# Cutting the last load of a DMA-bound elementwise kernel in two and holding the first store until the larger piece has landed

## The chip, the cores and the metric

The kernel runs on one core of one Trainium2 chip. The metric is device time in microseconds (us) of one execution, the median over the runs. The profile's span starts at the first DMA issue and is about 1.3 us shorter than the device time.

## The reference

Two float32 arrays of 1024 x 4096 are multiplied, and the tanh form of GELU is applied.

```python
def reference(x, y):
    z = x * y
    return (0.5 * z * (1 + np.tanh(np.sqrt(2 / np.pi) * (z + 0.044715 * z ** 3)))).astype(np.float32)
```

That is 2 x 16.78 MB to read and 16.78 MB to write, with one multiply (VectorE) and one activation (ScalarE) per element.

## The kernel before

Every tensor is seen as 128 partitions x 32768 columns. x stays whole in SBUF (the core's own memory; the arrays lie in HBM, the chip's large memory) and is overwritten by the product and then by the result. y goes through a ring of 16384 columns. All DMAs are issued by the sync engine (SP) on one queue, in this order: first half of x, first half of y, second half of x, third quarter of y, last quarter of y, first half of the result, second half of the result. `_hoist` moves the first two loads to the front of the program.

```python
X_LOADS = [(0, 16384), (16384, 32768)]
Y_LOADS = [(0, 16384, 0), (16384, 24576, 0), (24576, 32768, 8192)]   # from, to, place in the ring
STEP = 4096
STORES = [(0, 16384), (16384, 32768)]
...
    _hoist(nc, [load_x(0).ins, load_y(0).ins])
    load_x(1)
    for i in (1, 2):
        nc.sync.wait_ge(sem_mul, (Y_LOADS[i][1] - Y_LOADS[1][0]) // STEP)
        load_y(i)
    # ... per y load and 4096 columns: tensor_mul, then Gelu activation in place ...
    for i, (a, b) in enumerate(STORES):
        nc.sync.wait_ge(sem_act, b // STEP)
        nc.sync.dma_start(out=out_r[:, a:b], in_=xs[:, a:b]).then_inc(sem_o[i], 16)
```

The first store needs only the fourth activation, so it enters the queue while the second half of the loads is still on its way, right behind the last y load.

## Time and profile before

| | kernel before |
|---|---|
| device time, median of 6 runs (range) | 120.86 us (120.66 to 120.92) |
| span of the profiled execution | 119.3 us |
| DMA queue in use | 98.7% of 16 engines' span |
| VectorE busy, ScalarE busy | 35.0 us, 30.2 us |
| bytes moved, mean rate | 50.33 MB, 422 GB/s |

The page's other lines are shown in the prediction. Two more views of the kernel before are used later. First the DMA issues by tensor (count, KB each, median us from issue to landing):

```profile
ys<-in_y_dram SPq DMA_DIRECT2D x2, 4096.0 KB, 21.0
xs<-in_x_dram SPq DMA_DIRECT2D x2, 40.3
out_dram<-xs SPq DMA_DIRECT2D x2, 31.8
```

Then what the sync engine waited for (total us, times, longest):

```profile
SPq L100 <- ACT xs L94: 33.7, 2, 30.4
SPq L105 <- DMA out_dram<-xs: 6.5, 1, 6.5
```

The stores wait for activations only. These two lines do not say whether a store that leaves early is good or bad; the time at which each transfer lands does. I read two kinds of records under the summary views: the **landing records** (one semaphore increment per DMA engine and transfer; I quote the last of the 16) and the **packet records** (start and length of each packet on a DMA engine). A transfer of 128 partitions is eight packets on each of the 16 engines, one per partition.

### The profile page before, as it was taken

How to read it: one execution, taken by the hardware profiler on the slowest of the kernel's cores; microseconds unless marked ns; L12 is line 12 of the kernel's file. 1: busy time of each engine (PE TensorE's matmuls, PEld its weight loads, DVE VectorE, ACT ScalarE, POOL GpSimd, SP SyncE). 2: the span in 40 equal slices, each digit the busy share in tenths (PEclk: the TensorE clock that was granted, in tenths of full speed). 3: DMA queues.
4: the chain of work that ended last, by engine and by line, in shares of the span. 5: the costliest groups of instructions: out<-in, count | busy, mean ns of one | idle time of the engine just before them, and what ended most of it. 6: DMA issues, size and time to landing. Idle time of an engine off the chain costs nothing.

```text
span 119.3 us, 68 instructions
## 1 busy us (share of the span) xinstructions
DVE 35.0 (29%) x8; ACT 30.2 (25%) x9; POOL 0.2 (0%) x4
## 2 busy tenths in 40 slices
DVE  0000000000000199999600049959990000000000
ACT  3000000000000006797790000977479200000000
POOL 0000000000000000000000000000000000000000
DMA  9899888998899889988898989998889888998894
GB/s 352 352 439 615 352 352 352 659 396 352 352 615 439 352 352 483 571 352 352 385 494 352 505 374 494 385 527 352 352 352 703 352 352 352 637 418 352 352 527 176
DMA packets 1008, 50.33 MB, mean 422 GB/s; under 512 B 112, under 2 KB 112, under 8 KB 112
## 3 DMA queue, kind: packets, MB, share of 16 engines
q1 hardware_dynamic: 1008, 50.33, 98.7%
HBM read 33.55 MB, written 16.78 MB: 422 GB/s over the span
## 4 chain that ended last, share of the span: by engine, by line
DMA 53%; DVE 22%; ACT 3%; SPq 0%; issue 0%; DVEq 0%
DMA ys<-in_y_dram 53%; DVE xs L87 22%; ACT xs L94 3%; SPq L66 0%; DVEq L85 0%
## 5 line engine op out<-in xcount | busy, mean ns | idle before, releaser
L87 DVE TENSOR_TENSOR xs<-xs,ys 128x4096 f32<-128x4096 f32 x8 | 35.0, 4420 | 54.5 <-DMA ys<-in_y_dram 54.5
L94 ACT ACTIVATE xs<-xs 128x4096 f32<-128x4096 f32 x8 | 28.9, 3617 | 61.0 <-DVE xs L87 61.0
L94 ACT ACT_TABLE_LOAD x1 | 1.3, 1283 | 1.9 <-PEq L54 1.9
L121 POOL MEMSET const-uint8-127<- 128x1 uint8 x1 | 0.1, 102 | 0.0
L121 POOL MEMSET const-bfloat16-1.0<- 128x1 bf16 x1 | 0.1, 101 | 0.0
L121 POOL MEMSET const-float32-0.0<- 128x1 f32 x1 | 0.1, 98 | 0.2 <-issue 0.2
L121 POOL MEMSET const-float32-1.0<- 128x1 f32 x1 | 0.1, 98 | 0.0
## 6 DMA issues: line engine op xcount, KB each, us to landing
ys<-in_y_dram SPq DMA_DIRECT2D x2, 4096.0 KB, 21.0
xs<-in_x_dram SPq DMA_DIRECT2D x2, 40.3
out_dram<-xs SPq DMA_DIRECT2D x2, 31.8
ys<-in_y_dram SPq DMA_DIRECT2D x1, 40.8
```

The source lines that it names most:

```text
L87: nc.vector.tensor_mul(out=xs[:, c : c + STEP], in0=xs[:, c : c + STEP], in1=ys[:, r + c - a : r + c - a + STEP],).then_inc(sem_mul, 1)
L94: nc.scalar.activation(out=xs[:, c : c + STEP], in_=xs[:, c : c + STEP], func=GELU).then_inc(sem_act, 1)
L121: nc = _bacc.Bacc("TRN2", target_bir_lowering=False, num_devices=1)
```

## The change

The intent: the store must no longer stand in the queue behind the loads, yet the queue must not run empty. So the last y load becomes 6912 + 1280 columns, and the first store is issued when the 6912 have landed; the 1280 columns keep the engines busy while the store is on its way to them.

```diff
-Y_LOADS = [(0, 16384, 0), (16384, 24576, 0), (24576, 32768, 8192)]
+Y_LOADS = [
+    (0, 16384, 0),
+    (16384, 24576, 0),
+    (24576, 31488, 8192),
+    (31488, 32768, 15104),
+]
...
-    for i in (1, 2):
-        nc.sync.wait_ge(sem_mul, (Y_LOADS[i][1] - Y_LOADS[1][0]) // STEP)
+    for i in range(1, len(Y_LOADS)):
+        nc.sync.wait_ge(sem_mul, -(-(Y_LOADS[i][1] - Y_RING) // STEP))
         load_y(i)
...
         for c in range(a, b, STEP):
+            w = min(STEP, b - c)
             # tensor_mul and activation of w columns instead of STEP
             n += 1
+            done[c + w] = n
...
     for i, (a, b) in enumerate(STORES):
-        nc.sync.wait_ge(sem_act, b // STEP)
+        if i == 0:
+            nc.sync.wait_ge(sem_y[-2], 16)
+        nc.sync.wait_ge(sem_act, done[b])
```

More of the change, by code (lines that the diff above doesn't have):

```diff
@@ L75 @@
     load_x(1)
-    for i in (1, 2):
-        nc.sync.wait_ge(sem_mul, (Y_LOADS[i][1] - Y_LOADS[1][0]) // STEP)
+    for i in range(1, len(Y_LOADS)):
+        nc.sync.wait_ge(sem_mul, -(-(Y_LOADS[i][1] - Y_RING) // STEP))
         load_y(i)
     n = 0
+    done = {}
     for i, (a, b, r) in enumerate(Y_LOADS):
@@ L86 @@
         for c in range(a, b, STEP):
+            w = min(STEP, b - c)
             nc.vector.tensor_mul(
-                out=xs[:, c : c + STEP],
-                in0=xs[:, c : c + STEP],
-                in1=ys[:, r + c - a : r + c - a + STEP],
+                out=xs[:, c : c + w],
+                in0=xs[:, c : c + w],
+                in1=ys[:, r + c - a : r + c - a + w],
             ).then_inc(sem_mul, 1)
             n += 1
+            done[c + w] = n
             nc.scalar.wait_ge(sem_mul, n)
             nc.scalar.activation(
-                out=xs[:, c : c + STEP], in_=xs[:, c : c + STEP], func=GELU
+                out=xs[:, c : c + w], in_=xs[:, c : c + w], func=GELU
             ).then_inc(sem_act, 1)
     for i, (a, b) in enumerate(STORES):
-        nc.sync.wait_ge(sem_act, b // STEP)
+        if i == 0:
+            nc.sync.wait_ge(sem_y[-2], 16)
+        nc.sync.wait_ge(sem_act, done[b])
         nc.sync.dma_start(out=out_r[:, a:b], in_=xs[:, a:b]).then_inc(sem_o[i], 16)
```

## The prediction

> **What bounds the kernel now.** I read the page first (its slices and its DMA part), then the chain of work that ended last, then the DMA landings of each tensor, and last the single packet records of the trace.
>
> ```profile
> span 119.3 us, 68 instructions
> DVE 35.0 (29%) x8; ACT 30.2 (25%) x9; POOL 0.2 (0%) x4
> DMA  9899888998899889988898989998889888998894
> q1 hardware_dynamic: 1008, 50.33, 98.7%
> HBM read 33.55 MB, written 16.78 MB: 422 GB/s over the span
> ...
> L87 DVE TENSOR_TENSOR xs<-xs,ys 128x4096 f32<-128x4096 f32 x8 | 35.0, 4420 | 54.5 <-DMA ys<-in_y_dram 54.5
> L94 ACT ACTIVATE xs<-xs 128x4096 f32<-128x4096 f32 x8 | 28.9, 3617 | 61.0 <-DVE xs L87 61.0
> ```
>
> The reader is to see that the 16 DMA engines are in use for 98.7% of the span, while VectorE and ScalarE work under a third of it. The kernel is one DMA queue that is never empty: 33.55 MB in, then 16.78 MB out. The slices look uneven only because whole packets are booked to a slice.
>
> The chain of waits names loads and multiplies, not the stores, and here it misleads about what is worth shortening:
>
> ```profile
> 58.77 21.87 DMA ys<-in_y_dram
> 80.64 0.03 issue
> 80.67 0.02 DVEq L85
> 80.69 0.04 issue
> 80.73 8.77 DVE xs L87 x2
> 89.50 0.02 issue
> 89.53 3.62 ACT xs L94
> ```
>
> The chain stops where the last activation ends, at 89.53 + 3.62 = 93.15 us. The second store is issued then, but the first store still holds the queue, as the landings by tensor show:
>
> ```profile
> L100 SPq DMA_DIRECT2D out_dram<-xs x2: 344/346/348, 62.4 to 93.2; - x2
> DMA to landing us min/median/max: 26.1/31.8/37.6
> ```
>
> The first store lands at 62.4 + 37.6 = 100.0 us, some 6.9 us after the second was issued, so the compute behind the last y load has 6.9 us of slack, and the second store follows without a hole (93.2 + 26.1 = 119.3 us).
>
> What can still be lost is in the queue itself. From the semaphore records, the last of each transfer's 16 landings is at 21.87 (x, first half), 41.21 (y, first half), 60.55 (x, second half), 70.27 (y, third quarter), 80.64 (y, last quarter), 99.97 (store 1) and 119.26 us (store 2). The differences are 19.34, 19.34, 9.72, 10.37, 19.33 and 19.29 us. A half is 8.39 MB and takes 19.34 us, so a quarter should take 9.67. The last y quarter, the one with a store queued right behind it since 62.4 us, takes 10.37: about 0.7 us too long. The packet records say where: a 32 KB load packet takes 1.213 us everywhere, but on all 16 DMA engines the seventh of the eight packets of that last load takes 1.83 to 2.17 us, starting at 76.6 to 77.1 us. The eighth is nearly normal again, and the store's first packets (2.418 us each, as later ones) follow without a gap. So the switch from loads to stores costs 0.6 to 0.95 us on an engine, and it is paid before the loads have ended. The only other loss is the first packet of the run (3.12 us on average against 2.42).
>
> **What the Trainium skill says.** "DMA: Bandwidth & Descriptors", section "Where 436 GB/s comes from", gives a ceiling of 435 GB/s; the stretch from 21.87 to 60.55 us moves 16.78 MB in 38.68 us, 434 GB/s, which agrees: there is nothing to win in the steady rate. The same page, section "Queues, rings and completion order", says that on each engine descriptors of a ring are consumed in order; the landing times above, in issue order, agree. The same page, "Latency and other measured facts", gives about 600 ns to the first byte of a load issued by the sync engine; here the first x load's issue ends at 0.38 us and its first packet starts at 1.00 us on the earliest engine and 1.48 us on the latest, so 0.62 us and more. I found no page that says what a change of direction in a queue costs.
>
> **The change, part by part.**
> 1. *The last y load is cut in two*, 6912 and 1280 columns. Both wait for the fourth multiply, so both are issued at about 58.8 to 59.2 us, behind a queue that is busy until 70.3. Bytes stay the same. Each load is eight packets per engine (one for each partition), so eight more packets. Two 32 KB packets take 2 x 1.213 = 2.426 us against 2.418 for one of 64 KB: 0.008 us per packet, 0.06 us for eight. No wait is added to the loads.
> 2. *Compute.* DVE work is split 4096, 2816 and 1280 in place of 4096 and 4096, the same columns in one more instruction. The 6912-column piece lands near 78.45 us (below), over 2 us before 80.64, so the last activation ends near 90 to 91 us instead of 93.15. All of it is in slack that the first store makes, and worth nothing.
> 3. *The first store waits for the 6912-column landing* instead of leaving at 62.4 us. This is the part that matters. It removes the stretched packet if that comes from the store standing behind the load: minus 0.7 us (10.37 - 9.67). It adds the risk of an empty queue. Packet time of the 6912 piece: 27/64 x 2.418 = 1.02 us, 8 packets, 8.2 us. The packets of the load before it end between 69.25 and 69.9 us according to the engine, so the piece's end at 77.4 to 78.1, and its last landing some 0.35 us later (as now, 80.30 to 80.64): 78.45. The sync engine passes a met wait in about 0.03 us (62.39 to 62.42 now), so the store is issued at 78.5. Its first packets can start 1.00 to 1.48 us later by the one start from an empty queue that the trace has: 79.5 to 80.0 us. Meanwhile the 1280 columns keep an engine busy for 8 x (5/64 x 2.418 + 0.004) = 1.5 us, to 79.0 to 79.6 us. The gap is then some 0.4 us, an estimate. The first store packet from an idle engine may also be slower than a queued one: the first load's was by 0.7 us, and a store reads from SBUF, so I take 0.15.
> 4. *Sum:* -0.7 + 0.06 + 0.4 + 0.15 = -0.1 us by this working. The odd width 1280 is just the length of the path from landing to first packet, which suggests that it was chosen for covering it; I therefore lean further to the gap being nearly closed and take -0.3 us: 120.87 - 0.3 = about 120.6 us.
>
> **The rivals.**
> A. *The switch itself costs what it costs.* If an engine must let its reads from HBM come home before it reads from SBUF, then 0.7 us of loss stays, moved behind the last load, and hides the late arrival of the store. For it: the start of the run shows a loss of the same size, 0.7 us. Against it: the stretched packet is the seventh, not a gap after the eighth. Result: 120.9 us.
> B. *The store comes too late.* The issue path takes its full 1.5 us, the first packet is 0.5 us slow, and nothing of it is covered: -0.7 + 0.06 + 0.5 + 0.5, up to 121.3 us. For it: 1.48 us on the slowest engine is measured.
> C. *The switch is free when the store comes just as the loads run out*, and the 1280 columns cover the path: the whole 0.7 us is won, 120.2 us. The floor for this queue is 119.3 - 0.7 of span, so nothing faster than about 120.1 us is to be had without touching the beginning.
> D. *The compute becomes the bound* through the extra instruction: it would have to eat 6.9 us of slack, and it gets about 2 us more of it. I give this nothing.
>
> **Range and chances.** A, B and C span 120.2 to 121.3, with most of the weight between A and C. I predict 120.6 us, and 120.1 to 121.1 for 8 in 10; runs of one kernel differ by 0.07 us, so noise adds little. Faster by over 2% means under 118.5 us, below the floor worked out above: 0.01. Slower by over 2% means over 123.3 us, a queue empty for more than 2.4 us: 0.02. The rest, 0.97, is within 2%.
>
> **What would show each step right or wrong.** The first store should be issued at 78.5 us and take some 21 us to land instead of 37.6. The seventh-packet stretch should be gone: the 6912-column piece should land 8.2 us after the y load before it, and no load packet should be over its normal length. Between the last 1280-column packet and the first store packet an engine should stand idle for 0 to 0.5 us; 0.7 us or more there speaks for A or B, and a first store packet well over 2.42 us for a slow start. If the stretch appears in the 6912 piece although no store is queued, then the store was not its cause. The second store must still be issued before the first lands, and land 19.3 us after it. The prediction is wrong in kind if the time is outside 120.1 to 121.1 us: below, if the steady rate of the loads or stores changes; above, if the queue stands empty for more than a microsecond.

## More of the kernel before

The record marks every execution reported here as fast, that is, not slowed, at a granted clock of 1.00. The experiments ran in four groups on four chips (e0 to e3; the widths; e8 to e10; e12). Each group had the kernel before beside it, with medians of 120.86, 120.91, 120.82 and 120.85 us, and the ratios are against these.

## The result

The changed kernel takes **120.13 us** (median of 6 runs, 120.05 to 120.39) against 120.86 us. The ratio is 0.9946, with a 95% interval of 0.9933 to 0.9959. Ratios here are the mean time of one kernel's fast runs over that of the other's fast runs of the same rounds, so they are not quite the ratio of the quoted medians. 0.9946 means 0.65 us saved (0.0054 x 120.86). This is inside the predicted range, but at its lower end.

The page of the changed kernel, to be held against the first fence of the prediction:

```profile
span 118.7 us, 73 instructions
DVE 34.9 (29%) x9; ACT 30.2 (25%) x10; POOL 0.2 (0%) x4
q1 hardware_dynamic: 1152, 50.33, 98.6%
HBM read 33.55 MB, written 16.78 MB: 424 GB/s over the span
```

Bytes and busy times are the same, there are 144 packets more (128 data packets and 16 semaphore writes for one more DMA), and the span is 0.6 us shorter. The share of 98.6% against 98.7% does not show where the time was saved: a packet that is held up counts as busy.

What the sync engine waited for, and the stores' issue and landing times, in the changed kernel:

```profile
SPq L110 <- DMA ys<-in_y_dram: 16.2, 1, 16.2
SPq L110 <- ACT xs L102: 11.7, 1, 11.7
...
L110 SPq DMA_DIRECT2D out_dram<-xs x2: 344/346/347, 78.5 to 90.6; - x2
DMA to landing us min/median/max: 20.9/24.5/28.1
```

The first store now waits 16.2 us for the y piece and leaves at 78.5 instead of 62.4 us. It then needs 20.9 us to land, not 37.6, because only the 1280 columns are in front of it.

The DMA issues of the changed kernel, for the y loads:

```profile
ys<-in_y_dram SPq DMA_DIRECT2D x1, 4096.0 KB, 20.2
ys<-in_y_dram SPq DMA_DIRECT2D x1, 3456.0 KB, 19.9
ys<-in_y_dram SPq DMA_DIRECT2D x1, 640.0 KB, 21.0
```

The landing records tell where the time went. The duration of a transfer is its last landing minus that of the transfer before it in the queue:

| transfer | before, lands at | duration | changed, lands at | duration |
|---|---|---|---|---|
| x, first half | 21.87 | | 21.75 | |
| y, first half | 41.21 | 19.34 | 41.08 | 19.33 |
| x, second half | 60.55 | 19.34 | 60.43 | 19.35 |
| y, third quarter | 70.27 | 9.72 | 70.14 | 9.71 |
| y, last quarter (both pieces) | 80.64 | **10.37** | 80.04 | **9.90** |
| store 1 | 99.97 | 19.33 | 99.39 | 19.35 |
| store 2 | 119.26 | 19.29 | 118.69 | 19.30 |

Of the 0.57 us between these two executions, 0.47 lie in the last quarter of y and 0.12 in the first landing, in which the two kernels do the same; a second profiled execution of the changed kernel (e0) had 22.09 us there. So the real gain lies in one place, where a queue of loads turns into a queue of stores.

### The profile page after: what moved, and what is told of

Its sections match the earlier page's. It is cut to its first block, busy times and chain, and to the rows that moved or that the text cites. A ratio compares the mean times of both kernels' runs of the same rounds, so it can differ in the third digit from the quotient of the medians.

```text
span 118.7 us, 73 instructions
## 1 busy us (share of the span) xinstructions
DVE 34.9 (29%) x9; ACT 30.2 (25%) x10; POOL 0.2 (0%) x4
## 3 DMA queue, kind: packets, MB, share of 16 engines
q1 hardware_dynamic: 1152, 50.33, 98.6%
## 4 chain that ended last, share of the span: by engine, by line
DMA 51%; DVE 18%; ACT 6%; issue 0%; SPq 0%; DVEq 0%
DMA ys<-in_y_dram 51%; DVE xs L94 18%; ACT xs L102 6%; SPq L71 0%; DVEq L91 0%
## 5 line engine op out<-in xcount | busy, mean ns | idle before, releaser
L94 DVE TENSOR_TENSOR xs<-xs,ys 128x4096 f32<-128x4096 f32 (+2 forms) x9 | 34.9, 3946 | 52.8 <-DMA ys<-in_y_dram 52.8
L102 ACT ACTIVATE xs<-xs 128x4096 f32<-128x4096 f32 (+2 forms) x9 | 28.9, 3235 | 58.5 <-DVE xs L94 58.5
```

The costliest lines, as they stand in the source:

```text
L94: nc.vector.tensor_mul(out=xs[:, c : c + w], in0=xs[:, c : c + w], in1=ys[:, r + c - a : r + c - a + w],).then_inc(sem_mul, 1)
L102: nc.scalar.activation(out=xs[:, c : c + w], in_=xs[:, c : c + w], func=GELU).then_inc(sem_act, 1)
```

## The experiments

Theory 1: a store that stands in the queue behind the loads holds their last packets up by 0.7 to 0.8 us, and the late store avoids it. Theory 2: the cut itself helps. Theory 3 (rival A of the prediction): turning from loads to stores costs this anyway. The column "last quarter" is the duration of the last y quarter by landing records, as above; undisturbed it should take 9.67 us, half of a half's 19.34.

| run | time, us | ratio (95%) | last quarter, us |
|---|---|---|---|
| kernel before | 120.86 | | 10.37 |
| e0, change repeated | 120.06 | 0.9935 (0.9923 to 0.9947) | 9.74 |
| e1, cut only | 120.77 | 0.9995 (0.9983 to 1.0007) | 10.36 |
| e2, uncut, store waits for the last y | 121.46 | 1.0052 (1.0040 to 1.0064) | 9.70 |
| e3, uncut, store waits for the third y | 120.87 | 1.0002 (0.9990 to 1.0014) | 10.45 |
| last piece of 768 columns | 120.90 | 1.0003 (0.9984 to 1.0022) | 9.94 |
| last piece of 1536 | 120.03 | 0.9933 (0.9918 to 0.9948) | 9.76 |
| last piece of 2048 | 120.00 | 0.9929 (0.9914 to 0.9945) | 9.82 |
| last piece of 2560 | 120.02 | 0.9928 (0.9911 to 0.9944) | 9.84 |
| e8, one more change of direction | 120.96 | 0.9999 (0.9972 to 1.0026) | 9.45 |
| e9, copy SBUF to SBUF in between | 125.16 | 1.0352 (1.0320 to 1.0385) | 10.72 |
| e10, copy HBM to HBM in between | 125.20 | 1.0356 (1.0324 to 1.0388) | 9.70 |
| e12, small early SBUF copy | 121.08 | 1.0012 (0.9998 to 1.0026) | 10.44 |

All outputs are right.

### e0: the changed kernel again

No edit; it was run beside the three below.

> The changed kernel itself, run on the same chip as the three experiments beside it, so that they have it for comparison. Every theory: 120.1 us, ratio to the kernel before 0.994 to 0.996; no load packet over its normal length before the first store; the loads end 9.9 us after the third y quarter.

It took 120.06 us, and the last quarter 9.74 us. On its engines the pause between the last load packet and the first store packet was 0.32 us on average in the packet records (0.18 in the first profiled execution). The pause is zero on the engine that ends its loads last. No load packet of the last quarter was long here (at most 1.03 us). In the first profiled execution some 27 KB packets took up to 1.18 us instead of 1.02, but at 70 to 75 us, far from the border; the engine that ended last lost 0.23 us there, which accounts for its 9.90 us.

### e1: the cut alone

```diff
     for i, (a, b) in enumerate(STORES):
-        if i == 0:
-            nc.sync.wait_ge(sem_y[-2], 16)
         nc.sync.wait_ge(sem_act, done[b])
```

> The last y load is cut into 6912 and 1280 columns, but the first store leaves at 62.4 us as in the kernel before. Theory 1 (the loss comes from the store standing in the queue behind the last load): the loss is back, 120.8 to 120.95 us, and some load packet near 77 us is 0.6 to 0.9 us too long. Theory 2 (the cut itself helps, by small last packets or earlier compute, and the store's wait does nothing): 120.1 us, no long packet. It also tells where the long packet lies: by count, it is the seventh of the eight 5 KB packets; by time, it is one that begins 1 to 2.4 us before the loads end, thus the last or last but one 27 KB packet.

It took 120.77 us, the time of the kernel before; the interval of the ratio includes 1. The DMA issues of e1 show the early store again, and the last piece half a microsecond slower than in the changed kernel (21.5 against 21.0):

```profile
ys<-in_y_dram SPq DMA_DIRECT2D x1, 640.0 KB, 21.5
xs<-in_x_dram SPq DMA_DIRECT2D x2, 40.4
out_dram<-xs SPq DMA_DIRECT2D x2, 33.1
```

The first 5 KB packets, which take 0.20 us in the changed kernel, take up to 0.65 us here, and some of the last 27 KB packets up to 1.43 instead of 1.02; the final four or so 5 KB packets are normal again. So the stall has a place in time, not in the count of packets. It begins 1.3 to 2.8 us before an engine's loads would have ended; the lengths of the packets do not bound it more closely. Theory 2 is out: the cut by itself wins nothing.

### e2: the wait alone

```diff
     for i, (a, b) in enumerate(STORES):
+        if i == 0:
+            nc.sync.wait_ge(sem_y[-1], 16)
         nc.sync.wait_ge(sem_act, b // STEP)
```

> The loads of the kernel before, uncut, and the first store waits until the last y load has landed. Theory 1: the long packet is gone (last y quarter 9.7 us instead of 10.37), but the queue is empty from landing plus issue: landing 0.35 us after the last packet, issue, and about 0.9 us to the first store packet as in the changed kernel (78.54 issue, 79.4 first packet), so a hole of 1.2 to 1.3 us; 120.86 - 0.7 + 1.25 = 121.4 us. Theory 3 (the change of direction costs 0.7 us anyway, hidden in the changed kernel by nothing): the hole is 1.3 us and the first store packet or the load still shows the 0.7 us, 122.1 us.

121.46 us, as theory 1 had it (121.4). The chain of e2 and its stores' landings:

```profile
58.79 21.21 DMA ys<-in_y_dram
...
L102 SPq DMA_DIRECT2D out_dram<-xs x2: 343/346/348, 80.0 to 92.5; - x2
DMA to landing us min/median/max: 20.8/24.2/27.6
```

The last y load takes 21.21 us from issue to landing, in place of 21.87, so the stall is gone. In exchange the queue is empty: the engines finish their loads at 79.0 to 79.6 us, the landing is complete at 80.00, the store is issued at 80.02, and its first packets start at 80.86 to 81.01. The mean pause of an engine is 1.68 us. This run also gives two sizes cleanly: **0.84 to 0.99 us from issue to first packet**, and 0.4 us from a load's last packet to its landing. A first store packet takes 2.45 us, nearly the usual 2.42.

### e3: a store that is issued later, but still early

```diff
     for i, (a, b) in enumerate(STORES):
+        if i == 0:
+            nc.sync.wait_ge(sem_y[-2], 16)    # loads uncut: the third y quarter
         nc.sync.wait_ge(sem_act, b // STEP)
```

> The loads of the kernel before, uncut, and the first store waits for the third y quarter, so that it is issued at 70.3 us rather than 62.4, with the last y load still wholly in front of it in the queue. Theory 1 in the form that any store queued in good time behind a load costs the load 0.7 us: 120.86 us, seventh packet long, no change. If what costs is how long the store has stood in the queue, or that it was issued during the earlier load: 120.2 us and no long packet.

120.87 us, no change, with the stall in place (10.45). The last y load, in the chain of e3:

```profile
58.93 21.95 DMA ys<-in_y_dram
```

A store issued at 70.4 us does the same harm as one at 62.4. Having stood 8 us less in the queue makes no difference.

### Other widths of the last piece

The edit is the same in all four, here for 2560:

```diff
-    (24576, 31488, 8192),
-    (31488, 32768, 15104),
+    (24576, 30208, 8192),
+    (30208, 32768, 13824),
```

> As the changed kernel, with a last piece of 768 columns in place of 1280, 0.6 us less of load behind the landing that lets the store go. The changed kernel's engines stood idle 0.0 to 0.6 us (mean about 0.3) between last load packet and first store packet. Theory 1: all of the 0.6 us becomes hole, 120.06 + 0.6 = 120.65 us. If the idle time costs nothing, 120.1 us.

> A last piece of 1536 columns, 0.3 us more of load behind the landing. If only the hole counts, its mean goes from 0.3 to about 0.1 us and the time to 119.9 us. If the stores that come a little early on some engines already hold their last loads up, no gain, 120.0 to 120.2 us.

> A last piece of 2048 columns, 0.9 us more of load than the changed kernel, so the store reaches the engines 0.4 to 0.9 us before their loads end. In the kernels with an early store the stall began 1.5 to 2.4 us before the loads would have ended. If a store may come as late as that without harm, no hole and no stall: 119.8 us. If the stall of 0.7 us comes back as soon as the store is there before the last load packet has ended: 120.5 to 120.8 us.

> A last piece of 2560 columns, 1.5 us more of load than the changed kernel: the store comes 1.0 to 1.5 us before the loads end. By the point at which the stall began in the kernels with an early store (1.5 to 2.4 us before the end), the stall should be mostly back: 120.5 to 120.9 us. If the loss depends on how long the store has stood in the queue, it is small still: 119.9 us.

With 768 columns the piece is too short. The store is issued at 79.63 us, its first packets start at 80.47 or later, and the engines pause 0.55 us on average, the last one too: store 1 lands 19.87 us after the last load, in place of 19.34. The 120.90 us are more than the 120.65 expected, with runs from 120.61 to 121.17; in the profiled execution the second x half and the third y quarter, which the width does not concern, took 19.58 and 9.90 us instead of 19.34 and 9.7. So I take only the loss of the gain as shown, not its exact size.

From 1280 to 2560 columns the time is flat: 120.13 and 120.06, 120.03, 120.00, 120.02 us. With 1536 or more the packet records show no pause at all. Yet the time is at most 0.06 us shorter than e0's (ratios 0.9928 to 0.9933 against 0.9935), so the pause that 1280 columns leave on the early engines cost next to nothing. My expectation that the stall would be back with 2560 was wrong. There the store was issued at 77.34 us; adding the 0.84 us of e2, it could start from 78.2, while the engines' loads ended at 79.5 to 80.0. So it stood ready some 1.3 to 1.8 us before their end and did no harm. A store that is ready about 8 us before the end (e3, 70.44 + 0.84 = 71.3 against 79 to 80) does the full harm. The limit lies between and was not located. The last piece of the 2048 run, issued at 59.0 us, lands free of the stall (20.9 us, against 21.5 for that of e1, issued at 59.2 us):

```profile
ys<-in_y_dram SPq DMA_DIRECT2D x1, 1024.0 KB, 20.9
```

Theory 3 falls here: with 1536 to 2560 columns the queue turns from loads to stores without a pause and without a stall.

### e9 and e10: which side of the transfer matters

Between the last y load and the first store a copy of 3584 columns is queued, which stays inside one memory. e9 copies SBUF to SBUF, so that behind the load only the memory that is read changes. e10 copies HBM to HBM, so that only the memory that is written changes.

```diff
+    spare = nc.alloc_sbuf_tensor("spare", [P, 3584], F32).ap()       # e9
+    spare = nc.dram_tensor("spare", [P, 3584], F32, kind="Internal").ap()   # e10
...
         nc.sync.wait_ge(sem_act, b // STEP)
+        if i == 0:
+            nc.sync.dma_start(out=spare, in_=xs[:, 0:3584]).then_inc(sem_e, 16)    # e9
+            nc.sync.dma_start(out=spare, in_=x_r[:, 0:3584]).then_inc(sem_e, 16)   # e10
```

> The kernel before with a copy from SBUF to SBUF of 3584 columns (1.84 MB, 4.23 us at the rate of 434 GB/s) queued between the last y load and the first store. Behind the load only the side that is read changes, from HBM to SBUF; the side written stays SBUF. If the stall comes from the change of what is read, the load's packets show it as before, before the copy, and the copy-to-store border shows none. If it comes from the change of what is written, the load is clean and the copy's packets show the stall before the store. Time 120.86 + 4.2 = 125.1 us either way.

> The mirror image: a copy from HBM to HBM of 3584 columns between the last y load and the first store. Behind the load only the side written changes, from SBUF to HBM. If the stall comes from the change of what is read, the load's packets are clean and the copy's packets show the stall before the store; if from the change of what is written, the load's packets show it. About 125.1 us either way, more if HBM to HBM is slower.

The last y load from issue to landing, in the chain of e9:

```profile
58.70 22.24 DMA ys<-in_y_dram
```

and in that of e10:

```profile
58.76 21.20 DMA ys<-in_y_dram
```

In e9 the load is held up (the seventh packet takes 1.74 to 2.23 us on the 16 engines, against 1.21), and the copy's packets before the store are all normal. In e10 the load is clean, and the stall, 0.88 us per engine summed over the packets, is mostly in the copy's fifth to seventh packets of eight (0.54 us each when undisturbed, up to 1.15 here); the eighth is normal. This answers the question for these four borders: the two at which what is **read** changes from HBM to SBUF have the stall, and the two at which only what is written changes have none. Both times are the 4.2 to 4.3 us longer that the copy's bytes cost.

### e8: one more change of direction

```diff
-STORES = [(0, 16384), (16384, 32768)]
+STORES = [(0, 4096), (4096, 16384), (16384, 32768)]
...
         load_y(i)
+        if i == 1:
+            store(0)      # behind the third y quarter, in front of the last
```

> The kernel before, but the first 4096 columns of the result are stored between the third and the last y load: two changes from load to store in the queue instead of one, and one back; same bytes, no hole by my arithmetic (last y lands near 86 us, second store issued near 99, first store ends near 100). If each change from load to store costs 0.6 to 0.7 us and the way back nothing: 120.86 + 0.65 = 121.5 us, with a long load packet before each of the two stores. If the way back costs as much: 122.2 us. If the loss comes only once in a run: 120.9 us.

120.96 us, ratio 0.9999: not one stall more, although the queue turns twice to stores. Of the expected times this is the one of a loss that comes only once in a run, which e12 tests next. The first turn has its stall (third y quarter 10.65 us instead of 9.7). The way back costs little: the small store lands 5.10 us after that quarter, against 4.84 for its bytes (a quarter of 19.34), and the y load behind it takes 9.45, less than 9.67; together that is 14.55 against 14.51. At the second turn the load packets are together only 0.08 us per engine too long. This contradicts the simple form of theory 1, by which every store standing behind loads costs 0.7 us.

### e12: is it paid once in a run?

A small copy from SBUF to SBUF is queued near 41 us, behind the first y load; the early store stays.

```diff
     _hoist(nc, [load_x(0).ins, load_y(0).ins])
+    nc.vector.memset(warm[:, 0:256], 0.0).then_inc(sem_w, 1)
+    nc.sync.wait_ge(sem_w, 1)
+    nc.sync.dma_start(out=warm[:, 256:512], in_=warm[:, 0:256]).then_inc(sem_e, 16)
     load_x(1)
```

> The kernel before with a small copy from SBUF to SBUF (256 columns, 0.13 MB, 0.3 us of the queue) between the first y load and the second x load, thus near 41 us in the queue; the early store is left as it was. The copy is the first read of SBUF by the DMA engines in this run. If the stall is paid once in a run, at the first read of SBUF behind loads (theory H1, from the run with two changes and one stall), it falls at about 39 us or vanishes, and no load packet near 77 us is long; time 120.86 + 0.3 = 121.2 us with the stall moved, 120.5 us if the small copy does not cost it. If the stall belongs to a change from loads to stores after a long stretch of loads alone (theory H2), the packets near 77 us are long as before, and the copy has a stall of its own or not: 121.2 to 121.9 us.

121.08 us. The last y load in the chain of e12:

```profile
58.77 22.31 DMA ys<-in_y_dram
```

The stall is still there (10.44 us; 0.74 us per engine in packets that start at 77 to 80 us), and at the small copy there is almost none (0.04 us per engine at 37 to 39 us). So it is not a cost of the first read of SBUF in a run. What remains open is why the small copy near 41 us and the second turn in e8 go nearly free, while the turns after the long stretch of loads (before, e1, e3, e9) and the first turn in e8 do not. e12 also differs by the size of what is read (1 KB packets), e8 by the shorter stretch of loads (9.7 us) between two stores; none of my runs separates the two.

## Why the prediction was right, and which of its terms were not

**What binds.** Right. The queue is the bound before and after; every transfer but the last y quarter has the same duration in the two kernels to 0.02 us.

**Where the loss sits and what removes it.** Right, and shown from both sides. The early store with the cut (e1) has it, the late store without the cut (e2) has not. Durations of the last quarter were 10.37 us before and 9.90 and 9.74 after. The working had minus 0.7; landings give minus 0.47 and minus 0.63 (the former with the 0.23 us that was lost early, see e0). One reading in it was too clean: in the kernel before, not every load packet ahead of the seventh took 1.213 us; some took up to 1.27.

**The times of the steps.** The larger piece was to land at 78.45 and landed at 78.52; the store was to be issued at 78.5 and was at 78.54; it took 20.9 us to land, for a predicted 21. The last activation was to end at 90 to 91 us, as the end of the chain after shows:

```profile
78.91 4.43 DVE xs L94
83.34 0.02 issue
83.36 7.22 ACT xs L102 x3
```

83.36 + 7.22 = 90.58 us, and the first store lands at 99.39, so the compute has 8.8 us of slack now and the extra multiply cost nothing (rival D).

**The terms that were mis-sized.** They are the hole and the slow first packet: "The gap is then some 0.4 us, an estimate" and "so I take 0.15". The estimate took 1.00 to 1.48 us from issue to first packet, from the start of the run; measured, it is 0.84 to 0.99 (e2), and 0.84 in the changed kernel (78.54 to 79.38). The late engines of the run's start do not come late again. A first store packet took at most 2.47 us, thus 0.05 more than usual, not 0.15.

The larger error is that the sum took the pause of an average engine (measured 0.18 and 0.32 us). A transfer has landed when its last engine has finished, and the engine that ended its loads last did not pause. What the pause and the slow packet cost together shows in the landing of store 1 after the last load: 19.35 and 19.37 us in the changed kernel against 19.33 before, thus 0.02 to 0.04 us in place of 0.55. In e2, where the last engine pauses too, it is 20.77. With 0.03 in place of 0.4 + 0.15, the sum is about minus 0.6 instead of minus 0.1 us, and the measured saving was 0.65 us (and 0.79 in e0, 0.0065 x 120.86). The lean to minus 0.3 came from the look of the width 1280 and not from working; it went the right way, half as far as needed.

**The rivals.** The result lies at rival C, 120.2 us, to which I gave too little. Rival A (the switch costs what it costs) is refuted by the widths of 1536 to 2560. Rival B (too late) is what happens with 768 columns and with e2, not with 1280. The floor of about 120.1 us holds to 0.1 us: the widths from 1536 to 2560, with neither pause nor stall, give 120.0.

**The number.** 120.6 us was predicted, 120.13 measured, inside 120.1 to 121.1 and within 2% of before. A wider last piece is no more than 0.1 us better, which the overlapping intervals do not resolve; I have no version that clearly beats the change.

## What to carry to other kernels

When a DMA queue is in use for 98% of the span, compare the landing times of equal transfers: an excess of 0.7 us in one of them showed a stall that the busy share cannot show. An early issue is not always free: here a store that stood ready 8 us or more ahead cost the loads in front of it 0.7 us, and one that stood ready only 1.3 to 1.8 us ahead cost nothing. This is no general law: the second turn of e8 was queued long ahead and was nearly free, for a reason that stays open. Give such a wait a small piece of work to hide behind, and choose it a little too large rather than too small: it must cover landing plus issue plus first packet (0.4 + 0.84 to 0.99 us here), after which the time was flat from 1280 to 2560 columns, while 768 lost the gain or most of it.

## What the Trainium skill lacked or had wrong

- "DMA: Bandwidth & Descriptors" says nothing of what a queue pays when it turns from loads to stores. By the landings it is 0.7 to 1.05 us here (before 0.70, e9 1.05), paid by the packets in front of the border when the transfer behind it reads SBUF and was queued long before (before, e1, e3, e9, e10, the first turn of e8). A transfer behind it that only writes elsewhere does not cause it (e9, e10). Its section "Two DMAs through the same engine are not ordered" says that an engine's read and write sides are separate queues. This fits a read side that reaches the border well before the write side, but no run here shows the inside of an engine, and the nearly free second turn in e8 and the small copy in e12 stay unexplained.
- The rule "Overlap DMA with compute" in that page's section "Rules for kernel authors" says to issue early and wait late, and names no exception. For the first store here, issuing at 62.5 us rather than 78.7 made an otherwise equal kernel 0.7 us slower (e1 against e0, 120.77 against 120.06).
- The same page's section "Anatomy of one DMA — SWDGE (gpsimd) path" gives a fixed cost of about 2.0 us per DMA, for that path; the page has no such sum for the path used here. For DMAs issued by the sync engine e2 shows 0.84 to 0.99 us from issue to first packet plus 0.4 us from last packet to landing, 1.2 to 1.4 us together. Its figure of about 600 ns to the first byte for this path ("Latency and other measured facts") agrees once the issue instruction's own 0.35 us is set aside: 0.49 to 0.64 us remain.
